# Block turns by way of DRAM in place of sixteen small copies and of 48 TensorE transposes, in a one-core RWKV-7 and HGRN2 layer

## The chip, the cores and the metric

One core of a Trainium2 chip runs the whole layer in one launch. The metric is the device time of that launch in microseconds (us). The kernel before took 1050.54 us (median of 3 runs, 1049.99 to 1050.96).

## The reference

The input x is 512 frames of 2048 values (fp32). One projection makes 8320 columns, of which 4224 go to eight pairs of RWKV-7 heads (64 wide, two to a tile of 128) and 4096 to eight HGRN2 heads (128 wide). Both branches are gated, put side by side, projected back to 2048 and normalized with the residual:

```python
proj = jnp.einsum('btd,dc->btc', h, w_in[l])
rw = _token_shift(proj[..., :RWKV_COLS], shift_mu[l]);  hg = proj[..., RWKV_COLS:]
# RWKV: per head a state S (64 x 64), one step for each frame
S = S * w_t + (S @ a_t) b_t^T + v_t k_t^T;   o_t = S @ r_t
o = group_norm(o) * gn_w + gn_b + sum(r * k * r_k) * v;   o_rwkv = o * silu(z)
# HGRN: gated linear recurrence, in chunks
S = S * f_t + k_t i_t^T;   o_t = q_t @ S
o_hgrn = rms_norm(o) * g_norm_w * silu(z)
y = concat([o_rwkv, o_hgrn]) @ w_out[l];   out = layer_norm(ALPHA * x + y)
```

## The kernel before, in words

**Matmuls.** Each large product is made in three passes of rounded fp32 (high by high, high by low, low by high); these are the matmuls of line 453 (`three`), and of line 1192 for the first three units. Weights come in pieces of 512 KB (tile `wr`, two buffers, line 430 in `load`), are split by ScalarE and VectorE into `wh` and `wl` (three buffers each, a quarter of a unit to a buffer), and `load(j+2)` is issued when the second quarter of piece j has been split. The input projection goes unit by unit, in the order k, r, v for each pair with z of the pair two before, then q and f of two heads, i (for four heads at once), and g. The output projection follows in four column blocks; in the first of them it takes the sixteen gated tiles in the order 0 to 5, 8 to 13, 14, 6, 15, 7, one in each twelve matmuls (`korder`, `split_gated`).

**The order of the work.** A planner (`Plan`) writes all engines' instructions out before the launch. It keeps a clock for each engine and lets generator threads (preparation of a pair, inversion and scan of a group of two pairs, two heads together, finishes, stores) put instructions between the matmuls of the projections when its clocks say that the operands are ready. On the chip each engine and SyncE's (SP's) DMA queue run their own list in order, held by semaphores alone. A thread that is late is simply put later; when a projection itself lacks something (weights, a free PSUM bank, a gated tile), the planner moves TensorE's clock on.

**Turning tiles.** RWKV's operands are made with channels on partitions and are needed with time on partitions. `turned` (line 392) does it for beta and k (tile `bk`, 128 x 8 x 128) and for v (128 x 8 x 64 into the lower half of `zz`): VectorE transposes each 32 x 32 block in place of its kind (line 366), and then SP's queue copies each block row to its place in SBUF with one DMA of 32 partitions (line 401): 16 DMAs for `bk`, 8 for v, in pieces of 128 bytes. After each four (or two) the thread waits some planned time. The other way, at the end of a pair (`rwkv_finish`) and of a head (`hgrn_out`), the normalized output goes back to channels on partitions by four TensorE transposes (line 328) of 128 x 128 into a PSUM bank, read by VectorE with the gain and the gate. `hgrn_out` also transposes three tiles of its keys.

**After the finish.** `put_gated` takes the finished tile `g`; twelve of the sixteen (pairs 0 to 5, heads 0 to 5, `SPILL`) are stored to DRAM (line 606) and read back when the output projection starts (line 1255). Tiles `g` have four buffers, tiles `t` eighteen. All finishes of pairs are in one planner queue, one after the other.

Of the kernel before, what the change touches and what calls it, by code (L numbers as in the profile page):

```python
# [15 lines left out]
P = 128  # L16
# [46 lines left out]
class Plan:  # L63
# [15 lines left out]
    def __init__(self, room):  # L79
        self.clock = {"pe": 0.0, "dve": 0.0, "act": 0.0, "pool": 0.0, "dma": 0.0}  # L80
# [65 lines left out]
    def fetched(self, tile, size):  # L146

        self.clock["dma"] = max(self.clock["dma"], self.clock["pe"]) + size * 128 / 360e3
        self.ready[tile.tensor.name] = (self.clock["dma"] + 2.0, "dma")

# [91 lines left out]
def mixer_kernel(ctx, tc, head, x_r, w_all, par, up, ln_wb, consts, hmask, out):  # L242
# [53 lines left out]
    def landed(*tiles):  # L296
# [9 lines left out]
        return test  # L306


    def size(ap):
# [81 lines left out]

    def turned(dst, src, tmp, rows=4, base=0):


        name = dst.tensor.name
        yield dtr(tmp, src)
        yield lambda: by_now(tmp)
        for a in range(4):
            for b in range(rows):
                o = base + 32 * b  # L400
                nc.sync.dma_start(dst[o : o + 32, :, 32 * a : 32 * a + 32],
                                  tmp[32 * a : 32 * a + 32, :, 32 * b : 32 * b + 32])
# [24 lines left out]
    def load(j):  # L427
        if j < nload:
            raws[j] = st("wr", [P, HALF])
            nc.sync.dma_start(raws[j], w_all[j - nhead])  # L430
            plan.fetched(raws[j], 4 * HALF)
# [116 lines left out]
    def constants():  # L548
        raw = st("ksq", [P, T])[:, : 16 * len(LEVELS)]
        for t, a in ((pr, par), (cst, consts), (raw, hmask)):  # L550
            nc.sync.dma_start(t, a)
# [48 lines left out]
    def put_gated(k, g):  # L600

        gated[k] = g
        if k in SPILL:
            def run():
                yield lambda: by_now(g)
                nc.sync.dma_start(spill[SPILL.index(k)], g)
                drop(g)

            plan.add(stores, run())
# [5 lines left out]
    def next_up():  # L615
        if len(ups) < NPAIR:
            upw = take("up", [P, 2, P])
            nc.sync.dma_start(upw, up[len(ups)])
            plan.fetched(upw, 8 * P)
            ups.append(upw)  # L620

    hc = [slice(64 * h, 64 * h + 64) for h in range(2)]

    def rwkv_prep(S, p):
# [114 lines left out]
        yield room(zz=1)  # L739
        z = take("zz", [P, NCH, P])  # L740
        yield room(ksq=1)
        tmp = take("ksq")
        yield from turned(z, chunks(v), chunks(tmp), rows=2, base=64)
        drop(v, tmp)
        S["zz"] = z

    def from_v(SS, sc):

        yield lambda: all("zz" in S for S in SS)
        zs = [S["zz"] for S in SS]  # L750
        yield room(main=2, mix=1)
        yield landed(*zs, sc)
        pss = [take("main") for _ in SS]
        for half, (z, ps) in enumerate(zip(zs, pss)):
            for c in range(NCH):
                for h in range(2):
                    yield mm(ps[hc[h], c * C : c * C + C], sc[64:128, 0, half * 16 + 2 * c + h],
                             z[64:128, c, hc[h]])

        def keep():  # L760
            for z, ps in zip(zs, pss):
                for h in range(2):
                    yield copy(z[0:64, :, hc[h]], chunks(ps[hc[h]]))
                drop(ps)

        return keep

    def outputs(SS, sc):
# [3 lines left out]
        for half, (S, po) in enumerate(zip(SS, pss)):  # L772
            z = S["zz"]
            yield lambda z=z: by_now(z)
            for c in range(0, NCH, 2):
                for h in range(2):
                    for e in range(2):
                        yield mm(po[hc[e], c // 2 * P + 64 * h : c // 2 * P + 64 * h + 64],
                                 sc[:, 1, half * 16 + 2 * (c + e) + h], z[:, c + e, hc[h]])
        for S, po in zip(SS, pss):  # L780
# [51 lines left out]
    def rwkv_scan(SS, sc):  # L832
# [9 lines left out]
        def block(ps, h):  # L842
            return ps[hc[h], h * 64 : h * 64 + 64]

        for rt, bds, o in zip(rts, bdss, os):
            yield memset(rt[64:128], 0.0)
# [4 lines left out]
        for c in range(NCH):  # L851
            more = c < NCH - 1
            zs = [zz[:, c] for zz in zzs]
            news = [bds[c % 2] for bds in bdss]
            pxs = []
            if c > 0:
# [5 lines left out]
                for rt, px, z in zip(rts, pxs, zs):  # L862
                    yield stt(rt[0:64], px[0:64, :P], -1.0, z[0:64], ALU.mult, ALU.subtract)
                if more:
                    for new, old, pc in zip(news, olds, pcs):
                        yield act(new, old, AF.Copy, scale=pc[:, c : c + 1])
            else:
                for rt, z in zip(rts, zs):
                    yield copy(rt[0:64], z[0:64], scale=-1.0)
            yield landed(*rts)  # L870
# [5 lines left out]
            for psa, z in zip(psas, zs):  # L876
                for h in range(2):
                    yield copy(z[0:64, hc[h]], block(psa, h))
                drop(psa)
# [17 lines left out]
    def rwkv_finish(S, p):  # L897
# [20 lines left out]
        yield landed(o_all)  # L918
        po = take("mix")
        for j in range(4):  # L920
            yield tr(po[:, j * P : j * P + P], o_all[:, j])
        yield act(sz, z, AF.Tanh, scale=0.5)
        yield stt(g, po, hcol(HGW, p), S["bv"], ALU.mult, ALU.add)
        drop(po)
        yield stt(z, sz, 1.0, z, ALU.add, ALU.mult)
        yield stt(g, g, hcol(HGB, p), z, ALU.add, ALU.mult)
        drop(z, S["bv"], S["ot"], sz)
        put_gated(p, g)

    def rwkv_group(SS, grp):  # L930
# [4 lines left out]
        def run():  # L935
# [121 lines left out]
    def hgrn_out(S, h, q, k, dt_, dg, tot, tots):  # L1057
# [37 lines left out]
        S["used"]()  # L1095
        yield landed(o2)
        pn = take("mix")
        for j in range(4):
            yield tr(pn[:, j * P : j * P + P], o2[:, j * P : j * P + P])
        yield has(S, "g")  # L1100
        yield stt(g, pn, hcol(HHW, h), S["g"], ALU.mult, ALU.mult)
        drop(S["g"], pn, o2)
        put_gated(8 + h, g)
# [28 lines left out]
    scans = [plan.queue(), plan.queue()]  # L1132
    groups, finishes, preps = plan.queue(), plan.queue(), plan.queue()
    heads, stores = plan.queue(), plan.queue()
# [13 lines left out]
    def fetch(k):  # L1148
        raw = firsts[k] = take("q4", [P, T + FIRST * P])
        if k:  # L1150
            nc.sync.dma_start(raw, head[k])
        else:

            nc.scalar.dma_start(raw[:, T:], head[k, :, T:])
            for c in (slice(0, T // 2), slice(T // 2, T)):
                nc.sync.dma_start(raw[:, c], head[k, :, c])
        plan.fetched(raw, 4 * size(raw))
# [90 lines left out]
    def reload(n):  # L1248
        while len(asked) < min(n, KT):
            k = korder[len(asked)]  # L1250
            asked.append(k)
            if k in SPILL:
                plan.until(lambda: gated[k] is not None and (plan.free("t") or plan.free("g")))
                gated[k] = take("t" if plan.free("t") else "g")
                nc.sync.dma_start(gated[k], spill[SPILL.index(k)])
                plan.fetched(gated[k], 4 * T)
# [104 lines left out]
    def finish(t):  # L1361
# [4 lines left out]
        def norm():  # L1366
            ahead = []
            for d in range(5):
# [5 lines left out]
                if d:  # L1374
                    y, b, o, k = ahead.pop(0)
                    yield keyed(tt(y, y, b, ALU.add), k, k)
                    nc.sync.dma_start(o, y)

# [8 lines left out]
    def finish_last(t, pbs, weigh):  # L1387
# [16 lines left out]
        def norm():  # L1404
# [8 lines left out]
            for d in range(4):  # L1413
# [3 lines left out]
                for c in (slice(0, T),) if d < 3 else (slice(0, T // 2), slice(T // 2, T)):  # L1417
                    if d < 2:
                        yield keyed(stt(y, y, rs, b, ALU.mult, ALU.add), k + k_r, k)
                    else:  # L1420
# [3 lines left out]
                                    kc + k_r + [p.tensor.name], kc)  # L1424
                    nc.sync.dma_start(o[:, c], y[:, c])

# [26 lines left out]
    def residual(t, d):  # L1453
        plan.until(room(g=1))
        xrs[t] = take("g")
        nc.sync.dma_start(xrs[t], x_r[t, :, d * T : d * T + T])
        plan.fetched(xrs[t], 4 * T)
# [8 lines left out]
    def ahead(j, d):  # L1466

        if d == 0:
            split_gated(j + 2)
            if j == 8:  # L1470
                plan.until(room(big=1))
                lnw.append(take("big", [P, 2, D]))
                nc.sync.dma_start(lnw[0], ln_wb[None].to_broadcast([P, 2, D]))
                plan.fetched(lnw[0], 8 * D)
# [192 lines left out]
```

## Time and profile before

| | us |
|---|---|
| median of 3 runs | 1050.54 |
| profiled execution, its own time | 1050.24 |
| its span, first to last instruction | 1048.5 |
| TensorE busy | 1040.6 |
| VectorE busy | 755.7 |
| ScalarE busy | 437.6 |

The profile is of one execution. TensorE's busy time counts from a matmul's start to its modelled end; matmuls overlap, so that the distance between two starts, not the duration, is what one costs. An fp32 matmul shows as two records, a transpose as one.

### The profile page before, as it was taken

How to read it: one execution, taken by the hardware profiler on the slowest of the kernel's cores; microseconds unless marked ns; L12 is line 12 of the kernel's file. 1: busy time of each engine (PE TensorE's matmuls, PEld its weight loads, DVE VectorE, ACT ScalarE, POOL GpSimd, SP SyncE). 2: the span in 40 equal slices, each digit the busy share in tenths (PEclk: the TensorE clock that was granted, in tenths of full speed). 3: DMA queues.
4: the chain of work that ended last, by engine and by line, in shares of the span. 5: the costliest groups of instructions: out<-in, count | busy, mean ns of one | idle time of the engine just before them, and what ended most of it. 6: DMA issues, size and time to landing. Idle time of an engine off the chain costs nothing.

```text
span 1048.5 us, 18840 instructions
## 1 busy us (share of the span) xinstructions
PE 1040.6 (99%) x7342; PEld 865.1 (83%) x7342; DVE 755.7 (72%) x1653; ACT 437.6 (42%) x867; POOL 38.3 (4%) x81
## 2 busy tenths in 40 slices
PE   9999999999999999999999999999999999999997
PEld 8888888888888888888888888888888888888885
DVE  7465898667759987676689866865998778625556
ACT  6545333445353354452533353525334554323321
POOL 0000000000000000000000000000000002000000
PEclk9999999999999999999999999999999999999999
DMA  8134342222343522223534323234352244545613
GB/s 332 54 103 114 99 109 86 86 79 81 84 123 100 122 82 74 78 98 79 138 78 118 98 62 96 70 96 110 100 128 72 69 164 131 182 131 159 202 60 131
DMA packets 87305, 114.79 MB, mean 109 GB/s; under 512 B 56368, under 2 KB 58160, under 8 KB 87088
## 3 DMA queue, kind: packets, MB, share of 16 engines
q1 hardware_dynamic: 87072, 113.39, 36.6%
q8 instruction: 58, 0.95, 0.4%
q14 instruction: 31, 0.25, 0.1%
q10 hardware_dynamic: 144, 0.20, 0.1%
HBM read 99.92 MB, written 7.34 MB: 102 GB/s over the span
## 4 chain that ended last, share of the span: by engine, by line
PE 99%; DVE 1%; DVEq 0%; issue 0%
PE main L453 74%; PE mix L324 11%; PE mix L453 8%; PE main L1192 3%; PE main L324 2%; PE mix L328 1%; PE mix L1142 0%; DVE inv L356 0%; DVE inv L347 0%; DVE stats L1549 0%; DVEq L1663 0%; DVE mv L1357 0%; DVE bd L356 0%; DVE mv L352 0%; DVE inv L1140 0%
## 5 line engine op out<-in xcount | busy, mean ns | idle before, releaser
L453 PE MATMUL main<-xl,wh 128*128 128x512 f32 x864 | 341.1, 395 | 0.0
L453 PE MATMUL main<-xh,wl 128*128 128x512 f32 x864 | 341.1, 395 | 0.0
L453 PE MATMUL main<-xh,wh 128*128 128x512 f32 x864 | 340.9, 395 | 0.0
L337 ACT ACTIVATE wh<-wr 128x512 fp32r<-128x512 f32 x299 | 186.9, 627 | 237.1 <-PE main L453 180.5
L347 DVE TENSOR_TENSOR wl<-wr,wh 128x512 fp32r<-128x512 f32 x299 | 203.8, 682 | 61.8 <-ACT wh L337 60.1
L453 PEld LDWEIGHTS main<-xh,wh 128*128 128x128 f32 x864 | 162.4, 188 | 33.0
L453 PEld LDWEIGHTS main<-xh,wl 128*128 128x128 f32 x864 | 162.5, 188 | 32.6
L453 PEld LDWEIGHTS main<-xl,wh 128*128 128x128 f32 x864 | 162.4, 188 | 32.6
L453 PE MATMUL main<-wl,xh 128*128 128x512 f32 (+1 forms) x262 | 102.6, 392 | 0.0
L453 PE MATMUL main<-wh,xh 128*128 128x512 f32 (+1 forms) x262 | 102.1, 390 | 0.0
L453 PE MATMUL main<-wh,xl 128*128 128x512 f32 (+1 forms) x262 | 101.6, 388 | 0.0
L453 PEld LDWEIGHTS main<-wh,xh 128*128 128x128 f32 x262 | 49.2, 188 | 9.9
L453 PEld LDWEIGHTS main<-wh,xl 128*128 128x128 f32 x262 | 49.2, 188 | 9.7
L453 PEld LDWEIGHTS main<-wl,xh 128*128 128x128 f32 x262 | 49.2, 188 | 9.6
L338 ACT ACTIVATE t<-main,om 128x512 f32<-128x512 f32 x33 | 22.4, 687 | 51.1 <-PE main L453 41.6
L356 DVE SCALAR_TENSOR_TENSOR t<-main,pr,t 128x511 f32<-128x511 f32 x33 | 24.4, 747 | 26.5 <-ACT t L338 26.2
L347 DVE TENSOR_TENSOR inv<-inv,inv 64x30 f32<-64x30 f32 (+14 forms) x120 | 38.6, 322 | 2.9
L347 DVE TENSOR_TENSOR inv<-inv 64x30 f32<-64x30 f32 (+14 forms) x120 | 38.4, 320 | 2.3
L347 DVE TENSOR_TENSOR t<-t,tot 128x256 f32<-128x256 f32 x96 | 37.8, 414 | 1.8 <-PE mix L324 1.7
L356 DVE SCALAR_TENSOR_TENSOR bd<-mix,pc,bd 64x64 f32<-64x64 f32 x112 | 31.7, 283 | 7.5 <-PE mix L324 5.2
L337 ACT ACTIVATE zz<-mix 64x64 f32<-64x64 f32 x63 | 13.8, 220 | 46.9 <-PE mix L324 45.8
L338 ACT ACTIVATE t<-main 128x512 f32<-128x512 f32 x32 | 18.5, 598 | 30.7 <-PE main L453 30.2
(222 smaller groups left out, 1328.0 us busy)
## 6 DMA issues: line engine op xcount, KB each, us to landing
wr<-w_all SPq DMA_DIRECT2D x156, 512.0 KB, 3.6
q<-head SPq DMA_DIRECT2D x15, 448.0 KB, 5.9
q<-q SPq DMA_DIRECT2D x128, 32.0 KB, 2.4
g<-x_r SPq DMA_DIRECT2D x16, 256.0 KB, 3.8
spill<-g SPq DMA_DIRECT2D x12, 256.0 KB, 2.7
out<-q SPq DMA_DIRECT2D x12, 256.0 KB, 2.4
t<-spill SPq DMA_DIRECT2D x10, 256.0 KB, 4.2
zz<-ksq SPq DMA_DIRECT2D x64, 32.0 KB, 2.6
```

What stands on the lines that cost most here:

```text
L324: return Op([("pe", cost, lambda: pe.matmul(o, l, r, start=start, stop=stop, **kw))], [l, r], [o], mode="narrow" if narrow else "main" if ...
L328: return Op([("pe", 0.11, lambda: pe.transpose(o, i, ident))], [i], [o])
L337: return "act", cost, lambda: sc_e.activation(o, i, f, scale=scale)
L338: return "act", cost, lambda: sc_e.activation(o, i, f, scale=scale, bias=bias)
L347: return dve_op([a, b], o, lambda: dve.tensor_tensor(o, a, b, f), base=0.16 if o.shape[0] < P and size(o) == C and o.tensor.name in tags e ...
L356: return dve_op([a, b], o, lambda: dve.scalar_tensor_tensor(o, a, s, b, f1, f2), per=0.00113, base=0.085 if o.shape[0] == P else 0.25 if s ...
L453: pe.matmul(ps, l, r, start=first and i == 0, stop=last and i == 2)
L1192: pe.matmul(pss[a], *ops, start=k == 0 and low == of == 0, stop=k == KT - 1 and low == 1)
```

## The change

`turned` keeps VectorE's block transpose, but writes it with the four block columns outermost; one DMA then stores the whole tile to a new DRAM tile `far`, and one DMA for each 32 destination partitions reads it back (4 for `bk`, 2 for v), in pieces of 1 KB (512 bytes for the finishes). The result has the order (block column, chunk, 32). For `bk` an added copy brings it into the old order in a second tile, which the scan now uses; `zz` is kept in the new order and its readers index it so. The ends of pairs 0 to 5 and of heads 0 to 5 use `turned` in place of the four transposes; pairs and heads 6 and 7 keep TensorE. The keys' transposes stay. Finishes of the two pairs of a group get a queue each. SP's issues get a planner clock (0.44 us each), from which planned landing times are now counted.

```diff
     def fetched(self, tile, size):
-        self.clock["dma"] = max(self.clock["dma"], self.clock["pe"]) + size * 128 / 360e3
-        self.ready[tile.tensor.name] = (self.clock["dma"] + 2.0, "dma")
+        self.clock["dma"] = max(self.clock["dma"], self.clock["sp"]) + size * 128 / 360e3
+        self.ready[tile.tensor.name] = (self.clock["dma"] + 1.8, "dma")
...
+    def send(o, i):
+        nc.sync.dma_start(o, i)
+        plan.clock["sp"] = max(plan.clock["sp"], plan.clock["pe"]) + 0.44
...
-    def turned(dst, src, tmp, rows=4, base=0):
-        name = dst.tensor.name
-        yield dtr(tmp, src)
-        yield lambda: by_now(tmp)
-        for a in range(4):
-            for b in range(rows):
-                o = base + 32 * b
-                nc.sync.dma_start(dst[o : o + 32, :, 32 * a : 32 * a + 32],
-                                  tmp[32 * a : 32 * a + 32, :, 32 * b : 32 * b + 32])
-            at = plan.clock["pe"] + 0.4 * rows
-            yield lambda: plan.clock["pe"] >= at
-        plan.ready[name] = (plan.clock["pe"] + 3.0, "dma")
+    def turned(dst, src, tmp, base=0):
+        c = src.shape[1]
+        n = src.shape[2] // 32
+        yield dtr(tmp, src.rearrange("p c (b f) -> p b c f", f=32))
+        yield lambda: by_now(tmp)
+        far = dpool.tile([4, 32, n, c * 32], F32, tag=nm("far"), name=nm("far"))
+        yield lambda: plan.clock["sp"] <= plan.clock["pe"]
+        send(far.rearrange("a p b r -> (a p) b r"), tmp.rearrange("p b c f -> p b (c f)"))
+        at = plan.clock["sp"] + 3.7
+        plan.busy[tmp.tensor.name] = (at, "dma")
+        yield lambda: plan.clock["pe"] >= at
+        for b in range(n):
+            yield lambda: plan.clock["sp"] <= plan.clock["pe"]
+            o = base + 32 * b
+            send(dst[o : o + 32].rearrange("p a c f -> p a (c f)"), far[:, :, b].rearrange("a p r -> p a r"))
+        plan.ready[dst.tensor.name] = plan.busy[dst.tensor.name] = (plan.clock["sp"] + 3.5, "dma")
...
         tmp = take("q4", [P, NCH, P])
-        yield from turned(bk, bk, tmp)
-        drop(tmp)
+        flat = bk.rearrange("p c t -> p (c t)")
+        yield from turned(blocks(flat, NCH), bk, blocks(tmp.rearrange("p c t -> p (c t)"), NCH))
+        yield copy(tmp.rearrange("p c (a f) -> p a c f", f=32), blocks(flat, NCH))
+        drop(bk)
+        S["bk"] = tmp
...
-        z = take("zz", [P, NCH, P])
+        z = take("zz", [P, 4, NCH, 32])
-        yield from turned(z, chunks(v), chunks(tmp), rows=2, base=64)
+        yield from turned(z, chunks(v), blocks(tmp, NCH), base=64)
...
             zs = [zz[:, c] for zz in zzs]
+            zs = [zz[:, :, c] for zz in zzs]
...
     def rwkv_finish(S, p):
-        yield room(g=1, ksq=1)
+        yield room(g=1)
         g = take("g")
+        if p < 6:
+            yield from turned(blocks(S["ot"], 4), o_all, blocks(g, 4))
+        yield room(ksq=1)
...
+        if p < 6:
+            yield act(in_blocks(g), blocks(S["ot"], 4).rearrange("p a c f -> p c a f"), AF.Identity,
+                      scale=hcol(HGW, p), bias=hcol(HGB, p))
+            yield act(sz, z, AF.Tanh, scale=0.5)
+            yield tt(g, g, S["bv"], ALU.add)
+        else:
+...
         yield stt(z, sz, 1.0, z, ALU.add, ALU.mult)
+        if p < 6:
+            yield tt(g, g, z)
+        else:
+            yield stt(g, g, hcol(HGB, p), z, ALU.add, ALU.mult)
...
-                plan.add(finishes, rwkv_finish(S, 2 * grp + i))
+                plan.add(finishes[i], rwkv_finish(S, 2 * grp + i))
...
     def hgrn_out(...):
+        if h < 6:
+            yield from turned(blocks(o2, 4), tiles(o2), blocks(g, 4))
+            yield has(S, "g")
+            yield act(in_blocks(g), blocks(o2, 4).rearrange("p a c f -> p c a f"), AF.Copy, scale=hcol(HHW, h))
+            yield tt(g, g, S["g"])
+        else:
+...
```

In the branches left out stand the four transposes and the multiply of before. `send` also takes the place of every other `nc.sync.dma_start`, and `from_v` and `outputs` read `zz` as `z[:, hb[h], c]`, where `hb[h]` are two blocks of 32.

## Rows read from the trace of the kernel before

**Rows 1.** page, the span and TensorE's busy time, share and instructions

```profile
span 1048.5 us, 18840 instructions
...
PE 1040.6 (99%) x7342; PEld 865.1 (83%) x7342; DVE 755.7 (72%) x1653; ACT 437.6 (42%) x867; POOL 38.3 (4%) x81
```

**Rows 2.** page, the chain of work that ended last, by line

```profile
PE main L453 74%; PE mix L324 11%; PE mix L453 8%; PE main L1192 3%; PE main L324 2%; PE mix L328 1%; PE mix L1142 0%; DVE inv L356 0%; DVE inv L347 0%; DVE stats L1549 0%; DVEq L1663 0%; DVE mv L1357 0%; DVE bd L356 0%; DVE mv L352 0%; DVE inv L1140 0%
```

**Rows 3.** longest wait of TensorE in the whole span: us, times, longest

```profile
PE mix L324 <- ACT ksq L1409: 1.5, 1, 1.5
```

**Rows 4.** line 328 (transposes): duration ns min/median/max, first and last start

```profile
L328 PE MATMUL mix<-cst,t x88: 270/272/328, 193.3 to 893.5; 128*128 128x128 f32 x88
```

**Rows 5.** timeline of TensorE around one lone group of transposes: start, us

```profile
892.98 0.39 PE L453 MATMUL main<-wh,xh 128*128 128x512 f32 x1
893.21 0.60 PE L328 MATMUL mix<-cst,t 128*128 128x128 f32 x4
...
893.88 0.40 PE L453 MATMUL main<-wh,xl 128*128 128x512 f32 x1
```

**Rows 6.** chain in order of time, 180 to 260: start, us, what

```profile
207.09 0.76 PE mix L328 x7
```

**Rows 7.** VectorE by line and shape: count, busy us, mean ns, idle before

```profile
L356 DVE SCALAR_TENSOR_TENSOR g<-mix,half,t 128x512 f32<-128x512 f32 x16 | 12.0, 747 | 9.0 <-PE mix L328 8.8
...
L366 DVE STREAM_TRANSPOSE q<-q 128x1024 f32<-128x1024 f32 x8 | 9.9, 1235 | 0.0
...
L366 DVE STREAM_TRANSPOSE ksq<-t 128x512 f32<-128x512 f32 x8 | 5.6, 701 | 0.0
```

**Rows 8.** ScalarE by line and shape

```profile
L338 ACT ACTIVATE t<-t,pr 128x512 f32<-128x512 f32 x8 | 5.7, 717 | 2.4 <-DVE t L356 2.4
```

**Rows 9.** SP's issues of line 401: duration ns, first and last start

```profile
L401 SPq DMA_DIRECT2D q<-q x128: 585/608/1292, 74.9 to 768.5; - x128
```

**Rows 10.** DMA issues: count, KB each, median us to landing

```profile
wr<-w_all SPq DMA_DIRECT2D x156, 512.0 KB, 3.6
...
spill<-g SPq DMA_DIRECT2D x12, 256.0 KB, 2.7
...
t<-spill SPq DMA_DIRECT2D x10, 256.0 KB, 4.2
...
up<-up SPq DMA_DIRECT2D x8, 128.0 KB, 3.2
```

**Rows 11.** SP's stores and reloads of gated tiles: duration ns, first and last start

```profile
L606 SPq DMA_DIRECT2D spill<-g x12: 326/329/430, 208.3 to 755.8; - x12
...
L1255 SPq DMA_DIRECT2D t<-spill x10: 319/404/433, 837.3 to 877.4; - x10
```

**Rows 12.** VectorE: block transposes and the last split of a gated tile: start, us

```profile
755.87 1.23 DVE L366 STREAM_TRANSPOSE q<-q 128x1024 f32<-128x1024 f32 x1
...
771.40 0.70 DVE L366 STREAM_TRANSPOSE ksq<-t 128x512 f32<-128x512 f32 x1
...
897.82 0.69 DVE L347 TENSOR_TENSOR xl<-g,xh 128x512 fp32r<-128x512 f32 x1
```

**Rows 13.** timeline of TensorE near 800 and 907: start, us

```profile
798.80 2.08 PE L324 MATMUL main<-zz,big 64*64 64x64 f32 x64
...
907.07 0.39 PE L453 MATMUL mix<-wh,xh 128*128 128x512 f32 x1
```

**Rows 14.** stretch: PE, PEld, DVE, ACT, POOL busy us (count), clock, DMA

```profile
740.00:800.00 60.00, 60.00 (x324) 49.52 (x324) 54.11 (x108) 19.11 (x32) 2.45 (x11) 1.00 0.40 112
```

**Rows 15.** inversion's matmuls in two short stretches

```profile
800.86:801.90 1.04, 1.04 (x64) 0.90 (x64) 0.00 (x0) 0.00 (x0) 0.00 (x0) 1.00 0.00 0
804.40:805.10 0.70, 0.70 (x64) 0.58 (x64) 0.00 (x0) 0.00 (x0) 0.00 (x0) 1.00 0.10 23
```

**Rows 16.** timeline of TensorE around a narrow group

```profile
804.02 0.39 PE L453 MATMUL main<-xh,wh 128*128 128x512 f32 x1
804.34 0.75 PE L324 MATMUL mix<-big,inv 32*32 32x32 f32 x64
```

More of the change, by code (lines that the diff above doesn't have):

```diff
@@ L79, in __init__ @@
     def __init__(self, room):
-        self.clock = {"pe": 0.0, "dve": 0.0, "act": 0.0, "pool": 0.0, "dma": 0.0}
+        self.clock = {"pe": 0.0, "dve": 0.0, "act": 0.0, "pool": 0.0, "sp": 0.0, "dma": 0.0}
         self.table = None
@@ L390, in copy, with in_blocks, blocks @@
         return Op([act_way(o, i, AF.Copy, scale), ("dve", 0.075 + size(o) * 0.00105 + moved(o, i), f)], [i], [o])
-    def turned(dst, src, tmp, rows=4, base=0):
-        name = dst.tensor.name
-        yield dtr(tmp, src)
+    def turned(dst, src, tmp, base=0):
+        c = src.shape[1]
+        n = src.shape[2] // 32
+        yield dtr(tmp, src.rearrange("p c (b f) -> p b c f", f=32))
         yield lambda: by_now(tmp)
-        for a in range(4):
-            for b in range(rows):
-                o = base + 32 * b
-                nc.sync.dma_start(dst[o : o + 32, :, 32 * a : 32 * a + 32],
-                                  tmp[32 * a : 32 * a + 32, :, 32 * b : 32 * b + 32])
-            at = plan.clock["pe"] + 0.4 * rows
-            yield lambda: plan.clock["pe"] >= at
-        plan.ready[name] = (plan.clock["pe"] + 3.0, "dma")
+        far = dpool.tile([4, 32, n, c * 32], F32, tag=nm("far"), name=nm("far"))
[9 more added lines that the diff above has]
+        plan.ready[dst.tensor.name] = plan.busy[dst.tensor.name] = (plan.clock["sp"] + 3.5, "dma")
+    def in_blocks(t):
+        return t.rearrange("p (c a f) -> p c a f", a=4, f=32)
+    def blocks(t, c):
+        return t.rearrange("p (a c f) -> p a c f", c=c, f=32)
     splits = plan.queue()
@@ L429, in load @@
             raws[j] = st("wr", [P, HALF])
-            nc.sync.dma_start(raws[j], w_all[j - nhead])
+            send(raws[j], w_all[j - nhead])
             plan.fetched(raws[j], 4 * HALF)
@@ L550, in constants @@
         for t, a in ((pr, par), (cst, consts), (raw, hmask)):
-            nc.sync.dma_start(t, a)
+            send(t, a)
             plan.fetched(t, 4 * size(t))
@@ L605, in run @@
                 yield lambda: by_now(g)
-                nc.sync.dma_start(spill[SPILL.index(k)], g)
+                send(spill[SPILL.index(k)], g)
                 drop(g)
@@ L617, in next_up @@
             upw = take("up", [P, 2, P])
-            nc.sync.dma_start(upw, up[len(ups)])
+            send(upw, up[len(ups)])
             plan.fetched(upw, 8 * P)
@@ L622, in mixer_kernel @@
     hc = [slice(64 * h, 64 * h + 64) for h in range(2)]
+    hb = [slice(2 * h, 2 * h + 2) for h in range(2)]
     def rwkv_prep(S, p):
@@ L757, in from_v @@
                     yield mm(ps[hc[h], c * C : c * C + C], sc[64:128, 0, half * 16 + 2 * c + h],
-                             z[64:128, c, hc[h]])
+                             z[64:128, hb[h], c])
         def keep():
@@ L762, in keep @@
                 for h in range(2):
-                    yield copy(z[0:64, :, hc[h]], chunks(ps[hc[h]]))
+                    yield copy(z[0:64, hb[h]], ps[hc[h]].rearrange("p (c a f) -> p a c f", c=NCH, f=32))
                 drop(ps)
@@ L778, in outputs @@
                         yield mm(po[hc[e], c // 2 * P + 64 * h : c // 2 * P + 64 * h + 64],
-                                 sc[:, 1, half * 16 + 2 * (c + e) + h], z[:, c + e, hc[h]])
+                                 sc[:, 1, half * 16 + 2 * (c + e) + h], z[:, hb[h], c + e])
         for S, po in zip(SS, pss):
@@ L843, in block, with by32 @@
             return ps[hc[h], h * 64 : h * 64 + 64]
+        def by32(t):
+            return t.rearrange("p (a f) -> p a f", f=32)
         for rt, bds, o in zip(rts, bdss, os):
@@ L852, in rwkv_scan @@
             more = c < NCH - 1
-            zs = [zz[:, c] for zz in zzs]
+            zs = [zz[:, :, c] for zz in zzs]
             news = [bds[c % 2] for bds in bdss]
@@ L862, in rwkv_scan @@
                 for rt, px, z in zip(rts, pxs, zs):
-                    yield stt(rt[0:64], px[0:64, :P], -1.0, z[0:64], ALU.mult, ALU.subtract)
+                    yield stt(by32(rt[0:64]), by32(px[0:64, :P]), -1.0, z[0:64], ALU.mult, ALU.subtract)
                 if more:
@@ L868, in rwkv_scan @@
                 for rt, z in zip(rts, zs):
-                    yield copy(rt[0:64], z[0:64], scale=-1.0)
+                    yield copy(by32(rt[0:64]), z[0:64], scale=-1.0)
             yield landed(*rts)
@@ L877, in rwkv_scan @@
                 for h in range(2):
-                    yield copy(z[0:64, hc[h]], block(psa, h))
+                    yield copy(z[0:64, hb[h]], by32(block(psa, h)))
                 drop(psa)
@@ L913, in rwkv_finish @@
         yield has(S, "z", "bv")
-        yield room(g=1, ksq=1)
+        yield room(g=1)
         g = take("g")
+        if p < 6:
+            yield from turned(blocks(S["ot"], 4), o_all, blocks(g, 4))
+        yield room(ksq=1)
         sz = take("ksq")
         z = S["z"]
[L918 to L924, printed above, removed]
+        if p < 6:
[4 more added lines that the diff above has]
+        else:
+            yield landed(o_all)
+            po = take("mix")
+            for j in range(4):
+                yield tr(po[:, j * P : j * P + P], o_all[:, j])
+            yield act(sz, z, AF.Tanh, scale=0.5)
+            yield stt(g, po, hcol(HGW, p), S["bv"], ALU.mult, ALU.add)
+            drop(po)
         yield stt(z, sz, 1.0, z, ALU.add, ALU.mult)
-        yield stt(g, g, hcol(HGB, p), z, ALU.add, ALU.mult)
+        if p < 6:
+            yield tt(g, g, z)
+        else:
+            yield stt(g, g, hcol(HGB, p), z, ALU.add, ALU.mult)
         drop(z, S["bv"], S["ot"], sz)
@@ L1095, in hgrn_out @@
         S["used"]()
[L1096 to L1102, printed above, removed]
+        if h < 6:
[3 more added lines that the diff above has]
+            yield tt(g, g, S["g"])
+            drop(S["g"], o2)
+        else:
+            yield landed(o2)
+            pn = take("mix")
+            for j in range(4):
+                yield tr(pn[:, j * P : j * P + P], o2[:, j * P : j * P + P])
+            yield has(S, "g")
+            yield stt(g, pn, hcol(HHW, h), S["g"], ALU.mult, ALU.mult)
+            drop(S["g"], pn, o2)
         put_gated(8 + h, g)
@@ L1132, in mixer_kernel @@
     scans = [plan.queue(), plan.queue()]
-    groups, finishes, preps = plan.queue(), plan.queue(), plan.queue()
+    groups, finishes, preps = plan.queue(), [plan.queue(), plan.queue()], plan.queue()
     heads, stores = plan.queue(), plan.queue()
@@ L1150, in fetch @@
         if k:
-            nc.sync.dma_start(raw, head[k])
+            send(raw, head[k])
         else:
@@ L1155, in fetch @@
             for c in (slice(0, T // 2), slice(T // 2, T)):
-                nc.sync.dma_start(raw[:, c], head[k, :, c])
+                send(raw[:, c], head[k, :, c])
         plan.fetched(raw, 4 * size(raw))
@@ L1254, in reload @@
                 gated[k] = take("t" if plan.free("t") else "g")
-                nc.sync.dma_start(gated[k], spill[SPILL.index(k)])
+                send(gated[k], spill[SPILL.index(k)])
                 plan.fetched(gated[k], 4 * T)
@@ L1376, in norm @@
                     yield keyed(tt(y, y, b, ALU.add), k, k)
-                    nc.sync.dma_start(o, y)
+                    send(o, y)
         plan.add(norms, norm())
@@ L1424, in norm @@
                                     kc + k_r + [p.tensor.name], kc)
-                    nc.sync.dma_start(o[:, c], y[:, c])
+                    send(o[:, c], y[:, c])
         plan.add(norms, norm())
@@ L1455, in residual @@
         xrs[t] = take("g")
-        nc.sync.dma_start(xrs[t], x_r[t, :, d * T : d * T + T])
+        send(xrs[t], x_r[t, :, d * T : d * T + T])
         plan.fetched(xrs[t], 4 * T)
@@ L1472, in ahead @@
                 lnw.append(take("big", [P, 2, D]))
-                nc.sync.dma_start(lnw[0], ln_wb[None].to_broadcast([P, 2, D]))
+                send(lnw[0], ln_wb[None].to_broadcast([P, 2, D]))
                 plan.fetched(lnw[0], 8 * D)
```

## The prediction

> **What bounds the kernel now.** I read the page's busy times first: TensorE is busy 1040.6 us of a span of 1048.5, VectorE 755.7, ScalarE 437.6 [rows 1]. The chain of work that ended last says the same by another way: all of it but a per cent is TensorE's lines, the projections at lines 453 and 1192 and the small matmuls between them [rows 2]. Third, the waits of TensorE: the longest is 1.5 us, on the last normalization at the very end [rows 3]; no wait for a DMA stands in that list. So TensorE runs without a gap from its first matmul to the tail, and a change is worth what it takes out of TensorE's list, less the gaps that it opens there. VectorE, ScalarE and SP's queue cost nothing until they make TensorE wait.
>
> **Transposes removed: 5.3 us less.** Line 328 holds 88 transposes: 4 for each of 8 pairs, 4 for each of 8 heads, 3 for each head's keys [rows 4]. The change takes out 6 x 4 + 6 x 4 = 48, in 12 groups of four. What a group costs is read from starts, not from durations: in a lone group the four start at 893.21, one projection matmul follows, and the next starts at 893.88, 0.67 us for four and one; an undisturbed matmul takes 893.21 - 892.98 = 0.23 us. The group costs 0.67 - 0.23 = 0.44 us, or 0.11 us each [rows 5]. Where seven stand together the chain gives 0.76 us, again 0.11 us each [rows 6], so a break in the projections adds little of its own, and it doesn't matter whether a removed group stood alone. 12 x 0.44 = 5.3 us, all on the path. Bounds: 0.33 us a group if the break's cost stays because other small matmuls keep it (4.0 us), 0.67 if the matmul behind it were dragged along (8.0 us).
>
> The Trainium skill, page "TensorE: Matmul & The Clock Gate", section "Part 4: PE-mode transpose", gives some 275 ns for a transpose of 128 x 128 in a kernel; the recorded duration here, 272 ns, agrees with that, the distance of 0.11 us between starts doesn't. By that figure 48 transposes would be worth 13.2 us. By the rows they overlap, and I go by the rows.
>
> **The ends of six pairs and six heads, by DMA.** Each gains a block transpose on VectorE, 0.70 us for 512 columns [rows 7], one ScalarE pass with gain and permuted reading, about 0.72 us [rows 8], one store and four reads; the multiply that reads PSUM, 0.75 us [rows 7], becomes one from SBUF of about the same length, so VectorE has 12 x 0.7 = 8.4 us more, ScalarE 12 x 0.7 = 8.6 us more. Latency of one: 0.70, an issue and landing of the store 2.7 (the spill's, the same 256 KB) [rows 10], four reads at 0.33 to 0.61 of SP each [rows 9, 11], the last landing after 3.2 to 4.2 [rows 10], ScalarE 0.72: about 9 to 11 us where four transposes took half of one. Who waits? The finished tile is stored and read back: the last store before is at 755.8, the first reload at 837.3 [rows 11]. That cover of 80 us hides 10; without it, each of the late ones would cost up to 10 us. Buffers `t` and `g` are held so much longer; no TensorE wait shows them short now, and I take zero, with 0 to 2 us as bounds (a unit of projection that waits once for one of these for a fifth of the 10 us).
>
> **Beta and k (`bk`), v (`zz`).** Sixteen issues of 0.61 us become five, eight become three [rows 9]. For `bk` the old path took 16 x 0.61 + 2.5 = 12 us; the new takes 2.7 to 3.6, four reads 1.3 to 2.4, a landing of 3.2 and the added copy (1.2 to 1.4 us, about two passes of 512): 8.5 to 11 us. No loss there. For v: 8 x 0.61 + 2.5 = 7.4 before, about 7 after. The tightest case is pair 7: its `bk` is turned by VectorE at 755.87, its v at 771.40 [rows 12], and the first matmuls that read the turned v run at 798.80 [rows 13]; 26 us of cover. The copies are eight, 8 x 1.2 = 10 us on ScalarE or VectorE.
>
> **SP's queue and the new waits.** SP issues 192 copies of 0.61 us now, 117 us of queue; then 8 x 5 + 8 x 3 + 12 x 5 = 124 at 0.33 to 0.61. New is that a read of `far` waits for the store before it, 28 times, and the weight loads behind it in SP's list wait too. The planner puts 3.7 us between, more than the 2.7 that a store takes, so a read should mostly find it landed. If not: a piece of weights feeds two quarters of 12 matmuls, 2 x 12 x 0.23 = 5.5 us, and is asked for three quarters (8.3 us) before its own split can start; it lands in 3.6 [rows 10]. Add the two quarters that TensorE has in hand, less 1.3 us for the split: it starves only if SP stands still for about 8.9 us. Cost 0, upper bound 28 x 0 for waits under that; were the cover gone, 28 x 2.7 = 76 us.
>
> **The last group.** This is the place where late work would be seen. Tile 7's split ends at 898.51 [rows 12]; it is needed 12 matmuls before 907.07 [rows 13], at 904.3. Slack 5.8 us. TensorE will be there 5.3 us sooner, but group 3's chain, which starts with pair 7's projections ahead of its turn at 755.87, moves forward with it by about 11 of the 12 groups, 4.9 us: 5.4 us of slack are left. Against that, VectorE is busy 54.1 of 60 us from 740 to 800 [rows 14], and four turns and two copies fall near it: 4 x 0.7 + 2 x 1.3 = 5.4 us at most. It just fits, and the two last finishes now run side by side. I take 0, bounds -0.5 and 3 us.
>
> **The reading of `zz` in blocks.** Matmuls now read rows of 2 or 4 runs of 32 values. The only rows near: inversion matmuls of 32 columns, the first kind reading single values 32 apart, 1.04 us for 64, the second reading a contiguous row, 0.70 for 64 [rows 15]: 5.3 ns for 32 jumps. By jumps, 112 records x 4 + 512 x 2 = 1472 jumps cost 0.25 us; by columns (112 x 128 + 512 x 64 = 47,100) 7.8 us. A run of 32 values is nearer to the contiguous row: I take 0.25.
>
> **The planner.** With other costs and an SP clock the small matmuls fall into other groups. Entering a narrow group costs about 804.34 - 804.02 - 0.23 = 0.09 us [rows 16], leaving it as much; ten groups more or fewer are 2 us. I take 0, with 2 us to either side.
>
> **Sum.** 1050.24 - 5.3 + 0.25 = 1045.2 for the profiled execution (span 1048.5 and 1.7 around it). The median of the runs lies 0.3 higher: 1045.5.
>
> **Rivals.**
> 1. *Reading `zz` in blocks costs by the column.* Slower: it decides from a price of 0.17 ns a column, 7.8 us; 1050.5 - 5.3 + 7.8 = 1053. For it: the inversion's row; against: that one jumps at each value. Chance 0.05.
> 2. *The last group comes late.* VectorE's and ScalarE's added work (27 us in the span) lands on the chain of group 3 and beyond the 5.4 us of slack each microsecond becomes a gap in TensorE; 10 us of it instead of 5.4 give back 4.6: 1050. For it: 90% busy before 800; against: it is 60 us long with 6 us free, and ScalarE only a third busy. Chance 0.14, a third of it slower than before (from 12.5 us on).
> 3. *A transpose is worth its duration*, 0.272 us, and nothing overlaps: 48 x 0.272 = 13.1, 1037.5. Against it stand four in 0.44 us. This is what the page's figure above would make of it. Chance 0.02; other gains over 8 us by regrouping 0.03.
> 4. *SP stands still for over 8.9 us* behind a store and the weights come late: 2 us a time at several of the 28 places, 1052. Chance 0.04.
>
> **How the numbers follow.** The forecast, a gain of 2 to 8 us, has 0.72; its own range is 1043 to 1047.5. About 0.2% (2.1 us) is what a measurement can tell from no change. Faster by more: 0.72 + 0.05 less 0.01 = 0.76; slower: 0.05 + 0.05 + 0.04 = 0.14; within: 0.10. The range that leaves out 2 in 10 reaches to the late group: 1042.5 to 1050.
>
> **What would show it.** Right: line 328 with 40 records; TensorE's busy time 1035 to 1036, gaps as small as before; the turned tiles' reads landing tens of microseconds before use; main matmuls 0.23 us apart. Wrong: a TensorE wait for a split or for weights (rivals 2, 4), in the window 840 to 905 above all; `zz` matmuls wider apart than the 2.08 us for 64 of now [rows 13] (rival 1); a pile of narrow groups (planner).

## The result, and the profile after

The changed kernel takes 1054.38 us as the median of six executions, one of which was slow (1150.90 us at a mean granted clock of 0.848) and is left out of everything below: the other five run from 1052.93 to 1057.66 with a median of 1053.79. The kernel before takes 1050.53. The ratio is 1.0039 with an interval of 1.0022 to 1.0055. It is slower, where 5 us less were forecast. The profiled execution is the slowest of the five, 1057.66 us with a span of 1055.9.

The page's first lines answer to [rows 1] and [rows 2]:

```profile
span 1055.9 us, 18747 instructions
...
PE 1041.6 (99%) x7294; PEld 865.0 (82%) x7294; DVE 758.1 (72%) x1657; ACT 455.1 (43%) x895; POOL 38.3 (4%) x81
...
PE 92%; DMA 3%; DVE 2%; ACT 1%; issue 1%; SPq 0%; DVEq 0%; ACTq 0%
```

TensorE has 48 matmuls less, as meant, and is still busy 1 us longer; the span less its busy time grew from 7.9 to 14.3 us. The chain that ended last isn't TensorE's alone any more: DMA, VectorE, ScalarE and "issue" stand in it, where the page of the kernel before has

```profile
PE 99%; DVE 1%; DVEq 0%; issue 0%
```

TensorE's longest waits (us in total, times, longest) show the new ones beside the tail's of [rows 3]:

```profile
PE mix L329 <- issue: 3.2, 2, 2.0
PE mix L329 <- DVE ksq L352: 2.0, 4, 1.3
PE mix L329 <- ACT ksq L1452: 1.5, 1, 1.5
PE mix L329 <- ACT ksq L342: 1.1, 1, 1.1
```

Line 1452 is the tail's wait, as before. New are the waits on `ksq` and two that nothing in the profile ends ("issue").

**The first loss** is seen on ScalarE and VectorE near 350 us (timelines: start, us, instruction, the idle time before it and what ended it):

```profile
345.25 0.63 ACT L342 ACTIVATE wh<-wr 128x512 fp32r<-128x512 f32 x1 [2.09 <-DVE inv L352]
349.87 1.06 ACT L342 ACTIVATE q<-q 128x1024 f32<-128x1024 f32 x1 [3.98 <-DMA q<-far]
350.83 0.61 ACT L342 ACTIVATE ksq<-t 128x512 fp32r<-128x512 f32 x1
```

```profile
351.48 0.69 DVE L352 TENSOR_TENSOR ksq<-t,ksq 128x512 fp32r<-128x512 f32 x1 [2.94 <-ACT ksq L342]
```

```profile
351.50 0.49 PE L329 MATMUL mix<-ksq,ones_r 128*128 128x512 f32 x1 [1.06 <-ACT ksq L342]
```

The copy of `bk` that the change adds is the first reader of the read-back. It stands 3.98 us in ScalarE's list until the read-back has landed, and everything behind it stands too. Next behind it is the high part of `ksq`, a split into two rounded parts of the product of r, k and `r_k`, which the same thread makes for two small matmuls. VectorE, which makes the low part, waits 2.94 us for it, and TensorE, whose list has come to the matmul, 1.06. At all four places below TensorE's wait is on `ksq`; none of its waits in this profile is on a split of weights (`wh`, `wl`). The landings of `bk` were longer than the planner's 3.7 us (store) and 3.5 us (read-back) (DMA issues: count, KB each, median us to landing; compare [rows 10]):

```profile
far<-q SPq DMA_DIRECT2D x8, 512.0 KB, 5.1
q<-far SPq DMA_DIRECT2D x32, 128.0 KB, 4.2
...
far<-g SPq DMA_DIRECT2D x12, 256.0 KB, 4.4
t<-far SPq DMA_DIRECT2D x48, 64.0 KB, 3.5
spill<-g SPq DMA_DIRECT2D x12, 256.0 KB, 4.2
```

**The second loss** is where TensorE waits for nothing, inside a run of small matmuls, and the clock falls behind it (stretches around 185 us: busy us and count of PE, PEld, DVE, ACT, POOL, granted clock, DMA share, GB/s):

```profile
184.00:185.40 1.40, 0.15 (x8) 0.00 (x0) 0.92 (x3) 0.00 (x0) 0.00 (x0) 0.70 0.00 0
185.40:188.00 2.60, 2.60 (x26) 2.14 (x27) 1.25 (x4) 1.92 (x5) 0.00 (x0) 0.50 0.03 6
188.00:190.00 2.00, 2.00 (x6) 1.52 (x6) 1.72 (x7) 0.83 (x3) 0.00 (x0) 0.50 0.00 0
190.00:192.00 2.00, 2.00 (x7) 1.36 (x5) 1.51 (x8) 0.00 (x0) 0.00 (x0) 0.65 0.00 0
192.00:194.00 2.00, 2.00 (x70) 1.69 (x70) 0.00 (x0) 1.11 (x3) 0.00 (x0) 1.00 0.00 0
```

0.50 is the 1.2 GHz level: after an idle stretch of 1.25 us the projection matmuls start 0.43 us apart instead of 0.23 for some 5 us.

The balance, from distances between the starts of projection matmuls (what exceeds 0.2275 us near each place): late splits at four places (350, 571, 724, 773 us) 1.73 + 0.45 + 0.34 + 1.46 = 4.0 us; waits without a cause 1.25 + 1.99, the slow clock behind them 2.56 + 1.07, together 6.9. With the 4.3 us that the transposes turned out to be worth (e6): 1050.2 - 4.3 + 4.0 + 6.9 = 1056.8 of 1057.7. These prices are readings of the trace; no run takes the second loss away and leaves the first.

### The profile page after: what moved, and what is told of

Same layout as the page of the kernel before. It is cut to its first block, busy times and chain, and to the rows that moved or that the text cites. A ratio compares the mean times of both kernels' runs of the same rounds, so it can differ in the third digit from the quotient of the medians.

```text
span 1055.9 us, 18747 instructions
## 1 busy us (share of the span) xinstructions
PE 1041.6 (99%) x7294; PEld 865.0 (82%) x7294; DVE 758.1 (72%) x1657; ACT 455.1 (43%) x895; POOL 38.3 (4%) x81
## 4 chain that ended last, share of the span: by engine, by line
PE 92%; DMA 3%; DVE 2%; ACT 1%; issue 1%; SPq 0%; DVEq 0%; ACTq 0%
PE main L470 68%; PE mix L329 11%; PE mix L470 8%; PE main L1235 3%; DMA q<-far 2%; PE main L329 2%; DMA far<-q 1%; DVE wl L352 1%; PE mix L333 0%; PE mix L1185 0%; DVE inv L361 0%; SPq L310 0%; DVE ksq L352 0%; ACT wh L342 0%; ACT L343 0%
```

## The experiments

Below, "late splits" stands for the first loss and "dry list" for the second. Some expectations on record put the first at 7.0 us; that counted the waits on `ksq` twice, and 4.0 is right. They also speak of late weight splits; in the changed kernel it is the split of `ksq`. Times are medians, with the ratio to the kernel before on the same chip.

**e1, e2, e3: take the wait off ScalarE.** In e1 the copy moves behind the turn of v; e2 adds a limit on runs of small matmuls; e3 leaves the copy in its place and gives it to GpSimd.

```diff
-        yield copy(tmp.rearrange("p c (a f) -> p a c f", f=32), blocks(flat, NCH))
...
         drop(v, tmp)
+        yield copy(bkt.rearrange("p c (a f) -> p a c f", f=32), blocks(flat, NCH))     # e1
...
+        yield Op([("pool", 3.2, lambda: pool.tensor_copy(po_, pi_))], [pi_], [po_])    # e3
...
             if e == "pe":
+                if self.run_of >= CAP:      # e2: 72; one more for each small matmul, 6 less for a projection's
+                    return False
```

> The changed kernel with one thing moved: the copy of bk stands behind the turn of v in its thread, some 8 us later, so that ScalarE does not reach it before the read-back has landed. Theory 'read-back' (ScalarE's copy waits 2 to 4 us in order for the read-back, and the weight splits behind it starve TensorE, 7.0 us in four places of the profiled execution): TensorE's waits on ksq vanish, 1046 to 1049. Its longest run of small matmuls is 176 records in 4 us where the changed kernel has 238 and 192 and the kernel before 167: theory 'dry list' (runs that long leave TensorE waiting for nothing that the profile shows, with a lower clock behind it, 6.9 us in that execution) leaves open whether a gap stays. Rival 'traffic' (the bytes by way of DRAM slow everything): still 1053 to 1055. Rival 'the transposes were worth nothing': 1050 at best.

> As e1, and the planner also lets no more than 72 small matmuls (144 records) stand together without projection matmuls between. Both theories: no wait on ksq, no wait without a cause, 1045 to 1046.5, the 5.3 us of the forecast. If e1 still has a gap without a cause, e2 is faster by that gap. Rival 'traffic': 1053 to 1055.

> The changed kernel with the copy of bk on GpSimd, where no weight split stands behind it; same place in the thread, same transfers. Theory 'read-back': ScalarE and VectorE no longer stand still, waits of TensorE on ksq gone, 1046 to 1048 (the copy itself takes longer there, which nobody waits for). Rival 'traffic', which does not care which engine copies: 1053 to 1055. Longest run of small matmuls 136 records: no wait without a cause by 'dry list'.

Measured: e1 1046.7 (0.9963, 0.995 to 0.9975), e2 1047.0 (0.9966), e3 1046.4 us (0.9961, 0.9949 to 0.9974). All three are faster than the kernel before. TensorE's waits in e3, the whole list:

```profile
PE mix L329 <- ACT ksq L1453: 1.5, 1, 1.5
PE mix L1186 <- DVE inv L1184: 1.1, 1, 1.1
PE mix L329 <- DVE ksq L352: 0.4, 1, 0.4
PE mix L333 <- DVE t L352: 0.3, 1, 0.3
```

The transfers are the same in e3 and only the engine of eight copies differs, so "traffic" falls. But e3's plan also has no dry list, so its 8 us are both losses; e1's runs of small matmuls, up to 168 records within 4 us, opened no gap either, which left e2's limit nothing to win.

**e4: `bk` turned as before,** the twelve ends and v by way of DRAM.

```diff
-        yield from turned(blocks(flat, NCH), bk, blocks(tmp.rearrange("p c t -> p (c t)"), NCH))
-        yield copy(tmp.rearrange("p c (a f) -> p a c f", f=32), blocks(flat, NCH))
+        yield from turned_old(bk, bk, tmp)
```

> The changed kernel with bk turned as in the kernel before (16 copies within SBUF, no read-back, no added copy); v and the twelve ends stay by way of DRAM. Theory 'read-back': 1045.5 to 1048, as e3; longest run of small matmuls 136, so no wait without a cause. Rival 'traffic': part of it goes with bk (8 of 28 turns, 8 of 17 MB), 1051 to 1053. Rival 'the transposes were worth nothing': 1050.5.

Measured: 1059.8 us (1.0081), the expectation missed by 12. The sixteen copies aren't counted on the planner's SP clock, and they stand ahead of the ends' read-backs in SP's list; ScalarE then waits for those instead (SP's timeline, then ScalarE's):

```profile
294.64 5.26 SPq L424 DMA_DIRECT2D q<-q  x8
300.00 1.49 SPq L310 DMA_DIRECT2D t<-far  x3
301.60 0.37 SPq L310 DMA_DIRECT2D wr<-w_all  x1
302.01 0.43 SPq L310 DMA_DIRECT2D t<-far  x1
```

```profile
307.07 0.81 ACT L343 ACTIVATE g<-t,half 128x512 f32<-128x512 f32 x1 [8.31 <-DMA t<-far]
```

```profile
PE main L483 <- ACT wh L342: 7.5, 4, 3.7
```

It is the same mechanism at another tile, 8.31 us in one wait, and here the weight splits (`wh`) stand behind it: TensorE waits 7.5 us for them. So e4 speaks for late splits, but says nothing on `bk` alone. It also has a wait without a cause, 1.1 us at 419.0, where none was expected.

**e5: the changed kernel again.**

> The changed kernel once more, for a second profile. 'Read-back': the same four places (near 351, 571, 724, 775) with TensorE's waits on ksq and late weight splits, some 7 us together, since they come from the lists' order. 'Dry list': the two waits without a cause near 185 and 616, each with a lower clock behind it, but their length may differ, because they hang on when the instruction fetch gets through; this is where runs of 1053 and of 1057 differ. 1053 to 1056. Rival: if the waits lie elsewhere, the story from one profile is chance.

Measured: 1054.7 us (1.0046). The same places: waits on `ksq` near 349, 568 and 772 (none at 724), waits without a cause at 184.8 (1.25 us) and 614.0 (2.28 us). Late splits come to 2.2 us here, the dry list with its clock to 6.0; 1050.6 - 4.3 + 2.2 + 6.0 = 1054.5. Of the two the dry list is the larger.

**e6: all ends on TensorE,** else as e1.

```diff
-        if p < 6:      # and h < 6
+        if p < 0:      # and h < 0
```

> e1 with all sixteen ends left on TensorE: only beta, k and v go by way of DRAM, the copy late. If 48 transposes are worth the 5.3 us of the forecast on the path, 1051.5 to 1052.5, 5.3 above e1 (1046.7); if the gain came from elsewhere (the planner's other order), 1046 to 1048.

Measured: 1050.9 us (1.0004, 0.9995 to 1.0013), 4.2 us above e1 by the medians and 4.3 by the ratios, or 0.09 us a transpose. The two intervals leave 2.7 to 5.9 us open, the forecast's 5.3 among them, and the difference is net of what the ends by DMA cost in e1. Beta, k, v, the new reading of `zz` and the SP clock together can't be told from no change.

**e7, e8: move the copy by what the planner thinks of the read-back** (changed kernel, 1.5 and 6.5 us for 3.5, for `bk` alone).

```diff
-        ... = (plan.clock["sp"] + 3.5, "dma")
+        ... = (plan.clock["sp"] + (1.5 if n == 4 and c == 8 else 3.5), "dma")   # e7; e8: 6.5
```

> The changed kernel with the planner told that bk's read-back lands 1.5 us after its last issue, not 3.5: the copy comes up to 2 us sooner in ScalarE's list and waits that much longer, eight times. 'Read-back': ScalarE's waits on the read-back grow by some 10 us in sum, TensorE's lost time by 4 to 10: 1057 to 1065. Rival 'the waits are hidden anyway and only the long runs of small matmuls cost': as before, 1053 to 1056, since its runs are as long (246 and 232 records).

> The changed kernel with the planner told that bk's read-back lands 6.5 us after its last issue: the copy waits no more. Its runs of small matmuls are as long as the changed kernel's (246 records near 612 and near 187). 'Read-back': no wait of TensorE on ksq. 'Dry list': waits without a cause at one or both of the runs of 246, with a lower clock behind them, and 2 to 5 us over e3 (1046.4). If these waits don't come, run length alone doesn't make them, and their cause stays open.

Measured: e7 1075.4 us (1.0231), more than expected; e8 1049.9 (0.9999, 0.9988 to 1.0009). ScalarE's waits on `far` in e7 first, then TensorE's waits in e8:

```profile
ACT q L342 <- DMA q<-far: 25.1, 5, 6.9
ACT g L343 <- DMA t<-far: 11.2, 4, 4.7
ACT q L342 <- DMA t<-far: 10.2, 2, 5.3
```

```profile
PE mix L329 <- issue: 4.0, 3, 1.6
PE mix L329 <- ACT ksq L1452: 1.5, 1, 1.5
PE mix L1185 <- DVE inv L1183: 1.0, 1, 1.0
```

In e7 TensorE's waits are

```profile
PE mix L329 <- ACT ksq L342: 8.5, 5, 4.0
PE mix L329 <- DVE ksq L352: 5.7, 8, 2.3
PE mix L329 <- issue: 3.8, 2, 2.2
```

A planned time that is 2 us sooner costs 21 us, most of it waits on `ksq` (14.2 us for 3.1); one that is late enough takes every such wait but the tail's away. The waits that are left in e8 are the dry list, 4.0 us; e8 took 3.5 us more than e3.

**e9: e8 with its runs cut** from 246 to 176 planned records. **e10, e11: e1 with the ends' read-backs thought 4.0 and 5.0 us long.**

```diff
+CAP = 88                                                                    # e9, 12 less for a projection's
...
-        ... = (plan.clock["sp"] + 3.5, "dma")
+        ... = (plan.clock["sp"] + (4.0 if c == 4 else 3.5), "dma")              # e10; e11: 5.0
```

> e8 with its longest runs of small matmuls cut by the planner from 246 records to 176 (no more than 88 small matmuls without projection matmuls between); bk's read-back thought as late as in e8. 'Dry list': no wait without a cause and no lower clock near 186 and 610, 1046 to 1048 against e8's 1049.9. Rival 'e8 is slow because its plan is' (its copy late, its buffers held): the waits may go, the time stays at 1049 to 1051.

> e1 with the planner told that the ends' read-backs (pairs and heads 0 to 5) land 4.0 us after their last issue, not 3.5. ScalarE's waits on t<-far (12.3 us in e1's profile) shrink by 2 to 4 us. As TensorE lost under 2 us to them in e1, 1045 to 1047: no change that can be told from e1.

> As e10 with 5.0 us: ScalarE's waits on t<-far under 5 us in sum; 1045 to 1046.5, up to 1 us under e1, if what is left of waits on late splits in e1 (some 1.6 us) goes and the plan opens no other gap.

Measured: e9 1050.6 us (1.0003): the wait near 186 went, one of 2.05 us at 607.5 stayed, so cutting runs wasn't enough. The time did not fall either, as the rival had it. In both kernels it goes with the granted clock (e9: 1048.6 us in the execution at 1.000, 1050.6 to 1052.2 in those at 0.996), but at 1.000 both still took 1048.5 us or more against e3's 1046.4. So how much of e8's 3.5 us over e3 is the dry list stays open. e10 is the fastest kernel, 1045.3 us (0.9952, 0.9939 to 0.9966); e11 took 1046.1 (0.9961, 0.9949 to 0.9974). Neither can be told from e1. e11 has a new wait without a cause, 1.4 us at 819.3. (The 12.3 us in e10's expectation are e3's; e1's waits on `t<-far` are 14.1.)

**e12, e13, e14: where in TensorE's list.** By then run length had failed: e9 has 208 records that start within 4 us near 182 without a wait, while e4 and e11 wait after 137 and 141 records in 4 us, no more than the 144 that the kernel before takes without one. Counted from the start of the list, the waits stand at fixed places. Here are the stretches that end just before them; the first count is TensorE's records so far. First the changed kernel, then e8:

```profile
0.00:185.35 185.35, 183.10 (x1244) 151.69 (x1244) 130.57 (x273) 84.24 (x145) 4.51 (x22) 1.00 0.43 138
0.00:616.63 616.63, 610.03 (x4534) 506.74 (x4535) 453.63 (x996) 280.42 (x543) 21.42 (x56) 0.99 0.39 118
```

```profile
0.00:185.07 185.07, 182.74 (x1116) 151.56 (x1117) 126.94 (x253) 86.97 (x148) 4.92 (x23) 1.00 0.44 138
0.00:606.96 606.96, 603.04 (x4277) 503.47 (x4277) 449.12 (x976) 281.00 (x538) 22.08 (x57) 1.00 0.40 120
0.00:824.61 824.61, 819.59 (x6047) 684.80 (x6047) 616.53 (x1357) 381.25 (x744) 30.63 (x73) 1.00 0.39 117
```

1244 - 1116 = 128, 4534 - 4277 = 2 x 128 + 1. By matmuls alone this holds for neighbours only (4277 - 1116 = 24 x 128 + 89), so the expectation's "all twelve" is too much. It holds throughout if TensorE's weight loads and the semaphore instructions in its list are counted too: the waits of the changed kernel then stand at places 2497 and 9152, those of e8 at 2240, 8641 and 12225, and all of them, the six of e12 to e14 included, are 192 or 193 past a multiple of 256. Next the list was moved with the plan untouched: small warm-up matmuls at the very start, 64 records more in e12 (on e8) and e14 (on the changed kernel), 128 in e13 (on e8).

```diff
-    WARM, T0 = 9, 4.2
+    WARM, TINY, T0 = 6, 35, 4.2          # e12, e14; e13: 3, 70
     for _ in range(WARM):
         pe.matmul(warm, zero, zero)
+    for _ in range(TINY):
+        pe.matmul(warm[0:32, 0:32], zero[0:32, 0:32], zero[0:32, 0:32])
```

> e8 with TensorE's list moved by 64 records: of the nine warm-up matmuls ahead of the first load three are left out, and 35 of 32 x 32 put in (70 records for 6). All else of the plan and of every list is e8's. 'Fetch by blocks': all twelve waits without a cause in seven profiles stand 128 records apart from each other or a multiple of that, so a block of the list is not there yet when TensorE comes to its end; moved by half a block, the runs of small matmuls fall otherwise, and e8's waits at records 1116, 4277 and 6047 (4.0 us, and 2.8 us of lower clock behind) go or move, each new one at half a block from the old places; 1046 to 1049 against 1049.9. Rival 'run length alone': the three waits stay where they are in the work, 1050.

> e8 with TensorE's list moved by 128 records (six warm-up matmuls out, 70 small ones in). 'Fetch by blocks': a whole block, so e8's three waits stay at the same matmuls of the work, 1049 to 1051. Rival 'any change at the start moves the times and the waits with it': the waits go or move.

> The changed kernel with TensorE's list moved by 64 records, as e12. 'Fetch by blocks': the waits at the runs near 185 and 616 (3.2 us, and 3.6 of lower clock in the first profile) go or move by half a block; the waits on ksq stay (3 to 7 us). If both go, 1050 to 1052 against 1054.4. Rival: 1054 to 1055, unchanged.

The stretches up to the waits in e12, e13 and e14:

```profile
0.00:185.23 185.23, 182.82 (x1116) 151.59 (x1117) 126.81 (x253) 86.52 (x148) 4.93 (x23) 1.00 0.43 138
0.00:609.06 609.06, 604.67 (x4405) 504.62 (x4405) 448.79 (x976) 281.02 (x538) 22.22 (x57) 1.00 0.39 119
```

```profile
0.00:192.36 192.36, 189.66 (x1244) 157.68 (x1245) 126.71 (x253) 87.00 (x148) 4.93 (x23) 1.00 0.41 133
0.00:614.24 614.24, 610.20 (x4405) 509.57 (x4405) 448.84 (x976) 280.61 (x538) 22.09 (x57) 1.00 0.38 118
0.00:830.58 830.58, 825.17 (x6175) 689.69 (x6175) 616.25 (x1357) 381.24 (x744) 30.64 (x73) 1.00 0.38 116
```

```profile
0.00:188.11 188.11, 185.85 (x1244) 153.76 (x1244) 128.84 (x270) 84.22 (x145) 4.50 (x22) 1.00 0.43 136
```

Moved by 128 (e13), all three of e8's waits stay in the work: 1116 + 128, 4277 + 128, 6047 + 128. Moved by 64, the first waits stay at the list's place (1116 in e12, 1244 in e14) and so fall 64 records earlier in the work; e12's second stands one block on (4405), 64 records later in the work; e8's wait near 824 and the changed kernel's near 616 are gone. The place in the list decides where a wait can stand. The changed kernel's page shows a queue of instructions (packets, MB, share):

```profile
q8 instruction: 57, 0.93, 0.4%
```

Its packets are 16 KB each, and TensorE's list of 7294 matmuls, as many weight loads and 158 other instructions makes one packet for some 256 instructions. In the profiles one of them starts 2.2 to 2.7 us before the end of every wait (all 18). So TensorE stands where the next block of its list hasn't arrived. The place alone isn't enough: of 901 blocks in the sixteen profiles, TensorE used 42 up in 3.2 us or less, the wait not counted; 18 of these end in the wait, and none of the others. Why the other 24 don't, no run shows.

The times, 1053.3 (e12), 1057.5 (e13) and 1058.6 us (e14), all missed what was expected. They carry a cost that the expectations left out: the small warm-up matmuls held up the first product, which starts at 6.7, 10.3 and 7.9 us for 5.3 in e8 and 5.0 in the kernel before, and its 144 matmuls took 35.5 us in e13 and 35.0 in e14 for 33.6 in e8. This doesn't account for all of e12's excess. The verdict of these three rests on places, not on times.

## Why the prediction was wrong

- **What bounds the kernel, and the transposes:** right. Line 328 became line 333 with 40 records, and e6 against e1 measures 4.2 to 4.3 us for the 48, between the bounds of 4.0 and 8.0, and not clear of 5.3. Without the two losses TensorE's busy time is 1035.8 (e1) and 1035.7 us (e3), as I had named.
- **`bk`: "No loss there" with "26 us of cover": the first step that failed.** I asked when TensorE reads the turned tiles and had 26 us; the first reader is the added copy, on ScalarE, right behind the transfer, and the split of `ksq` for TensorE's next small matmul is queued behind it. I priced it by its length, 10 us beside other work, and not by what its wait holds up. The landings were too short as well: 2.7 to 3.6 and 3.2 us taken, 5.1 and 4.2 measured. It cost 2 to 4 us in the profiled executions. e1, e3, e7 and e8 show it.
- **SP's queue:** the worry there was weights that come late behind a blocked read. The weights were in time, and in the changed kernel so were their splits as far as TensorE's waits show; it was another split on ScalarE, that of `ksq`, that came late. In e4 SP's list did stand, and ScalarE passed it on to the weight splits.
- **The planner: "I take 0, with 2 us to either side": the second step that failed,** and the larger one, 6 to 7 us in the profiled executions. I priced a change of order by the turns between kinds of matmul [rows 16]. What it did was to put longer runs of small matmuls (256 and 192 records, where the kernel before has 132 at most) where a block of the list ends. Whether an order does that is chance as far as the planner goes: e1, e2, e3, e6 and e10 have no such wait, e11 has one. No row of the kernel before has one, and none would have given its price.
- **Rivals.** None of the four is what happened. The late last group (rival 2) didn't show: waits ended by 775 us but for the tail. The turned reading of `zz` (rival 1) cost nothing: its three kinds of matmul are busy 17.2, 8.3 and 8.3 us before and after, and 64 in a row take 2.08 us at 808.44 as in [rows 13]. Transposes at full duration (rival 3) fell with e6. SP (rival 4) is answered above.
- **What I named as signs** worked: 40 records at line 333, and TensorE waits that the kernel before didn't have, though not between 840 and 905.

## What to carry to other kernels

When an operation is put behind a transfer, ask who stands behind it on its engine, and give it to an engine on which nobody does, or place it later; with the same eight copies the kernel took 1046.4 us with them on GpSimd (e3), and with a hopeful landing time for them on ScalarE 1075.4 (e7), with a late one 1049.9 (e8). When a change reorders many small matmuls, look for waits with no releaser, count all of TensorE's instructions up to them, and see whether the places differ by whole blocks. And a planner's landing times should be measured in the new traffic, not taken from the old.

## What the runs showed of the hardware

TensorE's list comes in blocks of 256 instructions (some 127 matmuls, their weight loads and a few semaphore instructions). Where a run of small matmuls reaches a block's end early, within 3.2 us of the one before, TensorE waited 1.1 to 2.3 us in 18 cases of 42. Behind the changed kernel's two, projections ran at a granted clock of 0.50, the 1.2 GHz level, for some 2 to 5 us; behind the single waits of e4 and e11 the clock stayed at 1.00. When a block is asked for, no run here shows. Also not expected: 140 records of 32 x 32 at the start took 7.6 us (e13), 54 ns each, where such records take 11 to 16 ns in the middle [rows 15].
